# Splitting the queries and keys of two heads on all 128 rows, and laying them over each other by DMA

## The chip, the cores and the metric

The kernel runs on one core of a Trainium2 chip. A time is that of one execution on the device in microseconds (us), the median of several runs; lower is better. The engines are TensorE (PE in the profile), VectorE (DVE), ScalarE (ACT), GpSimd (POOL) and SyncE (SP). Each takes its instructions in order, and semaphores make one wait for another. SBUF is the memory on the core, PSUM holds the results of TensorE in eight banks of 128 rows by 512 floats.

## The reference

Two blocks of a network on 512 tokens of width 2048, in float32. The first is a pooling mixer with a modulation; the second has three attention branches, a gate and an output projection. The change touches the split of queries and keys in two of the branches, of which this matters:

```python
# 64 wide heads: branch A has 12 query and 4 key heads (window), branch B 12 of each (forgetting)
q = rms_norm_2(q, q_gain); k = rms_norm_2(k, k_gain)
A: scores = einsum('bnqkgd,bnskd->bnkgqs', qb, kb) * d**-0.5 + bias        # window of 128, sinks
B: sc = einsum('bqhd,bshd->bhqs', qb, k) * d**-0.5 + cq - c                # causal, c = cumsum(log_f)
out = einsum('...qs,...sd->...qd', softmax(scores), v)
```

## The kernel before

Every float32 product is made of products of high and low parts: a value is cast to float32r (high) and the rest is what the cast left over (low). The stream of weights works like this: SP loads a piece of 128 x 1024 (line 53 and on), ACT casts it to `whi` (line 91), DVE subtracts to `wlo` (line 92), and TensorE multiplies high by high, low by high and high by low (`mm3`, line 260). Two halves of a piece are kept ready beyond the one in use (`take`, line 116). One half serves four banks of output, 12 matmuls.

Beside the projections run the attention units as generators. `aside` puts a generator into a lane, `step` (line 241) is called after every few projection matmuls and adds the lane's rate to a credit; at 1 the generator runs to its next `yield` (rate 0.41 for the units, line 1263). What it issues there stands in each engine's queue at that place. So the order on every engine is fixed when the program is built: a generator with fewer yields comes sooner. There are a unit of kind C, two of kind A (6 heads each) and three of kind B (4 heads each); `drain` ends a unit before the next one's inputs are done.

A unit begins with the head norm (`head_norm`, line 844; L862 and L867 multiply by the norm), then it transposes two heads of 64 at a time: four 128 x 128 transposes on TensorE (L888) into a bank of PSUM, s2 or s3 in turn (line 885), the first head in rows 0 to 63, the second in rows 64 to 127. `transp_stack` (line 882) casts and subtracts from there into the tile `qk12` (12 slots of 128 x 512). For queries a slot holds one head's high part in 64 rows and its low part in the other 64; for keys (kind B only) one slot holds the high part twice, another the low part twice. So one matmul over 128 rows gives high by high plus low by high. Each cast (L892, and L894 for the second copy of keys) and each subtraction (L896) works on 64 rows; an engine can write to other rows than it reads. Keys of kind A go through `transp_split` (L877, L879, L880), whose source has the head doubled already, so it works on all rows; the two calls of a unit take banks s2 and s3 in the same turn.

After that the scores follow (`s0`, line 1049, matmuls at L258 that read `qk12`), the exponentials (L1089), their transposes (`s2`, line 1098, L1111) and the split of the result into `pth` and `ptl` (L1136, L1138), of which there is one tile each (lines 1104 and 1105, 128 x 1280), and the product with the values (`s4`). The profile leaves numbers out of names, so `qk12` and the unsplit input `qk` are both called qk, and the banks s0 to s3 are all s.

Of the kernel before, what the change touches and what calls it, by code (L numbers as in the profile page):

```python
# [8 lines left out]
F32R = mybir.dt.float32r  # L9
AF = mybir.ActivationFunctionType  # L10
# [4 lines left out]
P = 128  # L15
D = 2048
T = 512
# [105 lines left out]
def build(tc, nc, x, vecs, bgate, fg, sinks, bforget, w_mod, w_pin, w_grp, w_pout, mem, w_in, w_kv,  # L123
          w_ba, w_bb, w_bc, w_out, ident, tri, dmask, rel, csel, edge, out):
    es = ExitStack()
    with es:
        _build(es, tc, nc, x, vecs, bgate, fg, sinks, bforget, w_mod, w_pin, w_grp, w_pout, mem, w_in, w_kv,
               w_ba, w_bb, w_bc, w_out, ident, tri, dmask, rel, csel, edge, out)


def _build(es, tc, nc, x, vecs, bgate, fg, sinks, bforget, w_mod, w_pin, w_grp, w_pout, mem, w_in, w_kv,
           w_ba, w_bb, w_bc, w_out, ident, tri, dmask, rel, csel, edge, out):
    V, S, PE = nc.vector, nc.scalar, nc.tensor
    mult, add, sub, vmax, vmin = ALU.mult, ALU.add, ALU.subtract, ALU.max, ALU.min

    def r32(ap):
        return ap.bitcast(F32)
# [85 lines left out]
    def bank(tag, name=None):  # L223
        return psp.tile([P, 512], F32, tag=tag, name=name or tag)
# [137 lines left out]
    b = bank("s3")  # L362
# [139 lines left out]
    for kp in range(8):  # L502
        if kp < 6:
            mem_pair(kp + 2)
        for c in range(2):
# [16 lines left out]
            w = st.whole()  # L522
# [293 lines left out]
    a3 = p3.enter_context(tc.tile_pool(name="a3", bufs=1))  # L816
# [65 lines left out]
    def transp_stack(srcs, outs, gain, keys):  # L882


        b = bank(S4[2 + nside[0] % 2])
        nside[0] += 1
        for i, s in enumerate(srcs):
            PE.transpose(b[:, i * P : (i + 1) * P], s, idf)  # L888
        for e in range(2):
            r, o = slice(64 * e, 64 * e + 64), slice(64 - 64 * e, 128 - 64 * e)  # L890
            hi = outs[e][0]
            S.activation(hi[r, :], b[r, :], AF.Copy, scale=gain[r, :])  # L892
            if keys:
                S.activation(hi[o, :], b[r, :], AF.Copy, scale=gain[r, :])  # L894
            for w in ((r, o) if keys else (o,)):
                V.scalar_tensor_tensor(out=outs[e][1][w, :], in0=b[r, :], scalar=gain[r, :], in1=r32(hi[r, :]), op0=mult, op1=sub)  # L896
            if e or keys:
                yield

    qk12 = a3.tile([P, 12, T], F32R, name="qk12")  # L900
    qkh, qkl = qk12[:, 0:6, :], qk12[:, 6:12, :]
    vhl = a3.tile([P, 2048], F32R, name="vhl")
# [50 lines left out]
    def attend(kind, unit, qk, vz):  # L953
# [12 lines left out]
        def head_state(h):  # L966
            if h not in hs:
                s = {}
                s["nm"] = a3.tile([P, NT], F32, tag="nm", name="nm", bufs=3)
                s["den"] = a3.tile([P, NT], F32, tag="den", name="den", bufs=3)  # L970
                if kind == "B" and "cs" not in s:
                    s["cs"] = a3.tile([P, T], F32R, tag="cst", name="cst", bufs=2)
                    S.activation(s["cs"], r32(ct2), AF.Copy, scale=csl[:, h0 + h : h0 + h + 1])
                hs[h] = s
            return hs[h]

        head_state(0)

        if kind == "C":
            vv = vhl.rearrange("p (m h e) -> p m h e", m=2, h=4)  # L980
# [6 lines left out]
        elif kind == "A":  # L987
            kd = [mkv[:, tt // 2, 512 + 256 * (tt % 2) : 768 + 256 * (tt % 2)].rearrange("p (j e d) -> p j e d", j=2, e=2) for tt in range(NT)]
            vv = vhl[:, :1024].rearrange("p (t h e) -> p t h e", t=NT, h=2)
            zoff = 128  # L990
            silu_z()
            yield from head_norm(qk, 0, 8, 64, k0=6, kdup=kd, beside=split_v([vz[:, tt, :128].rearrange("p (h e) -> p h e", e=64) for tt in range(NT)], [vv[:, tt] for tt in range(NT)], 64))
            for h in range(3):
                outs = [(qk12[:, 2 * h + e, :],) * 2 for e in range(2)]
                yield from transp_stack([qk[:, tt, h * P : (h + 1) * P] for tt in range(NT)], outs, gains[:, 0:1], False)
            for j in range(2):
                transp_split([kd[tt][:, j].rearrange("p a b -> p (a b)") for tt in range(NT)], qk12[:, 6 + 2 * j, :], qk12[:, 7 + 2 * j, :],
                             cols[:, R_KA : R_KA + 1])
                yield
        else:  # L1000
            vv = vhl.rearrange("p (t h e) -> p t h e", t=NT, h=4)
            zoff = 256
            silu_z()
            yield from head_norm(qk, 0, 8, 64, beside=split_v([vz[:, tt, :256].rearrange("p (h e) -> p h e", e=64) for tt in range(NT)], [vv[:, tt] for tt in range(NT)], 64))
            for h in range(4):
                hd = [2 * (h % 2) + e for e in range(2)]
                outs = [(qk12[:, 4 + i, :], qk12[:, 8 + i, :]) if h > 1 else (qk12[:, i, :],) * 2 for i in hd]
                g = gains[:, 1:2] if h < 2 else cols[:, R_KB : R_KB + 1]
                yield from transp_stack([qk[:, tt, h * P : (h + 1) * P] for tt in range(NT)], outs, g, h > 1)
# [242 lines left out]
    for (c0, n), ev in zip(CG[1:], (ev1, ev2)):  # L1252
        cb = [bank(t) for t in M4]
        for kp in range(8):
            tok_tile(cb, 2 * kp, h_h, h_l, kp == 0, kp == 7, n=n, evac=ev)
    drain()
    aside(attend("C", 0, qk, vz), 0.34)
    for kind, unit in (("A", 0), ("A", 1), ("B", 0), ("B", 1), ("B", 2)):
        qk2 = new_qk()
        proj(qk2, False)  # L1260
        vz2 = new_vz()
        proj(vz2, True)
        aside(attend(kind, unit, qk2, vz2), 0.41)
# [153 lines left out]
```

## Time and profile before

| | us |
|---|---|
| median of 3 runs | 2262.62 (2258.87 to 2263.61) |
| the profiled execution | 2262.3 |
| its span, first to last instruction | 2260.5 |
| TensorE busy | 2210.4 (98%) |
| DVE busy | 1146.5 (51%) |
| ACT busy | 883.5 (39%) |
| POOL busy | 0.2 (0%) |

The span is what the profile covers; the execution's own time is 1.8 us longer. Busy time is that of instructions at work. Matmuls overlap, so their durations (0.39 us for 512 columns) are longer than their spacing. In a row, "L892 ACT ACTIVATE qk<-s,gains" is line 892 of the kernel, the engine, the operation, output and inputs; "[0.97 <-DVE qk L896]" says that the engine was idle for 0.97 us before it, and what ended that. SPq is SP's queue of DMA issues.

### The profile page before, as it was taken

To read this page: it belongs to the slowest core of one execution; us is meant where nothing else is said; L and a number is where in the kernel's file an instruction comes from. 1 tells how busy PE (TensorE), PEld (TensorE's weight loads), DVE (VectorE), ACT (ScalarE), POOL (GpSimd) and SP (SyncE) were. 2 spreads that over 40 slices of the span, in tenths; PEclk is the share of its full clock that TensorE was granted. 3 is DMA by queue.
4 is the path that set the end of the run, shared out by engine and by line. 5 is a ranking of instruction groups with operands and counts; after the bars stand their busy time and mean duration, and the time that the engine had idled before them with its cause. 6 is when DMAs were issued, how large, how long until landed. Compare 5 with 4: busy or idle time off the path is not lost.

```text
span 2260.5 us, 26829 instructions
## 1 busy us (share of the span) xinstructions
PE 2210.4 (98%) x10199; PEld 1819.0 (80%) x10199; DVE 1146.5 (51%) x1997; ACT 883.5 (39%) x1719; POOL 0.2 (0%) x4
## 2 busy tenths in 40 slices
PE   7999999999999999999999999999999999999999
PEld 4678888888889988787778787788888888888887
DVE  3676665346665454757564645554334235326333
ACT  4433363333334354545464646442232222224221
POOL 0000000000000000000000000000000000000000
PEclk9989999999999999999999999999999999999999
DMA  9856633347674322222222222233333333333543
GB/s 334 276 164 217 202 99 98 94 122 231 225 224 120 105 75 75 75 75 75 75 75 75 75 75 75 66 98 99 94 93 103 96 100 94 102 94 98 154 131 112
DMA packets 164809, 275.12 MB, mean 122 GB/s; under 512 B 11090, under 2 KB 63048, under 8 KB 164424
## 3 DMA queue, kind: packets, MB, share of 16 engines
q1 hardware_dynamic: 164680, 273.41, 39.6%
q8 instruction: 80, 1.31, 0.2%
q14 instruction: 49, 0.40, 0.1%
HBM read 264.98 MB, written 8.39 MB: 121 GB/s over the span
## 4 chain that ended last, share of the span: by engine, by line
PE 82%; DVE 7%; ACT 5%; DMA 3%; issue 2%; SPq 0%; DVEq 0%; ACTq 0%
PE m L258 53%; PE s L258 26%; DVE wlo L92 2%; DVE qk L896 1%; DMA raw<-w_kv 1%; ACT pt L1089 1%; PE s L1111 1%; ACT whi L91 1%; DMA raw<-w_pout 1%; ACT qk L892 1%; DVE nm L1082 1%; DVE pt L1080 0%; DVE ptl L1138 0%; DVE acc L452 0%; PE colb L258 0%
## 5 line engine op out<-in xcount | busy, mean ns | idle before, releaser
L92 DVE TENSOR_TENSOR wlo<-raw,whi 128x512 fp32r<-128x512 f32 (+2 forms) x740 | 493.4, 675 | 759.6 <-ACT whi L91 744.7
L91 ACT CAST whi<-raw 128x512 fp32r<-128x512 f32 (+2 forms) x740 | 441.4, 608 | 872.5 <-PE m L258 385.4
L258 PE MATMUL m<-whi,h_h 128*128 128x512 f32 (+2 forms) x960 | 373.3, 389 | 1.7 <-ACT whi L91 1.1
L258 PE MATMUL m<-wlo,h_h 128*128 128x512 f32 (+2 forms) x960 | 363.0, 378 | 2.9 <-DVE wlo L92 2.6
L258 PE MATMUL m<-whi,h_l 128*128 128x512 f32 (+2 forms) x960 | 362.6, 378 | 0.0
L258 PE MATMUL m<-h_h,whi 128*128 128x512 f32 x768 | 304.2, 396 | 0.0
L258 PE MATMUL m<-h_h,wlo 128*128 128x512 f32 x768 | 301.4, 392 | 1.2 <-DVE wlo L92 1.2
L258 PE MATMUL m<-h_l,whi 128*128 128x512 f32 x768 | 301.1, 392 | 0.0
L258 PEld LDWEIGHTS m<-wlo,h_h 128*128 128x128 f32 x960 | 181.1, 189 | 31.9 <-DVE wlo L92 6.1
L258 PEld LDWEIGHTS m<-whi,h_l 128*128 128x128 f32 x960 | 180.7, 188 | 31.5
L258 PEld LDWEIGHTS m<-whi,h_h 128*128 128x128 f32 x960 | 181.2, 189 | 28.6 <-ACT whi L91 1.4
L258 PE MATMUL s<-h_h,whi 128*128 128x512 f32 x512 | 200.8, 392 | 0.0
L258 PE MATMUL s<-h_l,whi 128*128 128x512 f32 x512 | 200.4, 391 | 0.0
L258 PE MATMUL s<-h_h,wlo 128*128 128x512 f32 x512 | 200.4, 391 | 0.0
L258 PEld LDWEIGHTS m<-h_h,wlo 128*128 128x128 f32 x768 | 145.4, 189 | 32.6 <-DVE wlo L92 1.7
L258 PEld LDWEIGHTS m<-h_h,whi 128*128 128x128 f32 x768 | 145.6, 190 | 30.3 <-ACT whi L91 0.5
L258 PEld LDWEIGHTS m<-h_l,whi 128*128 128x128 f32 x768 | 145.5, 190 | 29.4
L258 PEld LDWEIGHTS s<-h_h,whi 128*128 128x128 f32 x512 | 97.1, 190 | 20.3
L258 PEld LDWEIGHTS s<-h_l,whi 128*128 128x128 f32 x512 | 97.0, 189 | 20.3
L258 PEld LDWEIGHTS s<-h_h,wlo 128*128 128x128 f32 x512 | 96.9, 189 | 20.3
L258 PE MATMUL m<-whi,y_h 128*128 128x512 f32 x256 | 102.6, 401 | 1.4 <-DVE t L778 1.4
L258 PE MATMUL m<-whi,y_l 128*128 128x512 f32 x256 | 99.9, 390 | 0.0
(239 smaller groups left out, 2739.6 us busy)
## 6 DMA issues: line engine op xcount, KB each, us to landing
raw<-w_mod SPq DMA_DIRECT2D x96, 512.0 KB, 4.3
raw<-w_in SPq DMA_DIRECT2D x96, 512.0 KB, 3.7
raw<-w_pin SPq DMA_DIRECT2D x58, 512.0 KB, 3.8
raw<-w_in SPq DMA_DIRECT2D x96, 256.0 KB, 3.0
raw<-w_pout SPq DMA_DIRECT2D x32, 512.0 KB, 4.4
raw<-w_out SPq DMA_DIRECT2D x32, 512.0 KB, 3.7
raw<-w_in SPq DMA_DIRECT2D x32, 384.0 KB, 3.4
raw<-w_kv SPq DMA_DIRECT2D x16, 512.0 KB, 6.6
```

What stands on the lines that cost most here:

```text
L91: self.nc.scalar.copy(h3, v)
L92: self.nc.vector.tensor_tensor(out=l3, in0=v, in1=h3.bitcast(F32), op=ALU.subtract)
L258: PE.matmul(ps, lhsT=lhsT, rhs=rhs, start=start, stop=stop)
L892: S.activation(hi[r, :], b[r, :], AF.Copy, scale=gain[r, :])
L896: V.scalar_tensor_tensor(out=outs[e][1][w, :], in0=b[r, :], scalar=gain[r, :], in1=r32(hi[r, :]), op0=mult, op1=sub)
L1082: V.tensor_reduce(out=s["nm"][:, qt : qt + m], in_=w, axis=AX.X, op=vmax)
L1089: S.activation(pt[:, c0 : c0 + n], (pt if kind == "A" else b)[:, c0 : c0 + n], AF.Exp, bias=s["nm"][:, qt : qt + 1], accum_out=s["den"][:, ...
L1111: PE.transpose(b[:, x * P : (x + 1) * P], pt[:, c : c + P], idf)
```

## The change

`transp_stack` now casts the whole bank, 128 rows, to a high part and subtracts on 128 rows to a low part. Both go into a free half of `pth` and `ptl` (columns 0 to 511 for the first pair of two, 512 to 1023 for the second); every other pair takes new tiles of these names, which are the same memory again. Then copies, started from POOL's queue, lay each head's 64 rows into `qk12`: two per head for queries, four for keys. There is one yield for every pair, where key pairs had two. Nothing else changes.

```diff
--- before.py
+++ after.py
@@ -886,17 +886,27 @@
         nside[0] += 1
         for i, s in enumerate(srcs):
             PE.transpose(b[:, i * P : (i + 1) * P], s, idf)
+        fresh = not both
+        if fresh:
+            both[:] = [a3.tile([P, 1280], F32R, tag=t, name=t) for t in ("pth", "ptl")]
+        c = slice(0, T) if fresh else slice(T, 2 * T)
+        hi, lo = both[0][:, c], both[1][:, c]
+        S.activation(hi, b, AF.Copy, scale=gain)
+        V.scalar_tensor_tensor(out=lo, in0=b, scalar=gain, in1=r32(hi), op0=mult, op1=sub)
+        if not fresh:
+            both.clear()
         for e in range(2):
             r, o = slice(64 * e, 64 * e + 64), slice(64 - 64 * e, 128 - 64 * e)
-            hi = outs[e][0]
-            S.activation(hi[r, :], b[r, :], AF.Copy, scale=gain[r, :])
             if keys:
-                S.activation(hi[o, :], b[r, :], AF.Copy, scale=gain[r, :])
-            for w in ((r, o) if keys else (o,)):
-                V.scalar_tensor_tensor(out=outs[e][1][w, :], in0=b[r, :], scalar=gain[r, :], in1=r32(hi[r, :]), op0=mult, op1=sub)
-            if e or keys:
-                yield
-
+                for w in (r, o):
+                    nc.gpsimd.dma_start(outs[e][0][w, :], hi[r, :])
+                    nc.gpsimd.dma_start(outs[e][1][w, :], lo[r, :])
+            else:
+                nc.gpsimd.dma_start(outs[e][0][r, :], hi[r, :])
+                nc.gpsimd.dma_start(outs[e][0][o, :], lo[r, :])
+        yield
+
+    both = []
     qk12 = a3.tile([P, 12, T], F32R, name="qk12")
     qkh, qkl = qk12[:, 0:6, :], qk12[:, 6:12, :]
     vhl = a3.tile([P, 2048], F32R, name="vhl")
@@ -975,6 +985,7 @@
             return hs[h]
 
         head_state(0)
+        both.clear()
 
         if kind == "C":
             vv = vhl.rearrange("p (m h e) -> p m h e", m=2, h=4)
```

Line 894 in the changed kernel is the cast, 895 the subtraction, 902 and 903 are the copies of keys, 905 and 906 those of queries; L1100 is what was L1089, L1147 what was L1136.

On ACT, in the first B unit, two query pairs and two key pairs are split between casts of the weight stream. Before:

```order
L892 ACTIVATE qk12_5578<-s2_9396,gains_74 64x512 [waits PE_49]
L892 ACTIVATE qk12_5578<-s2_9396,gains_74 64x512 [waits DVE_49]
L892 ACTIVATE qk12_5578<-s3_9411,gains_74 64x512 [waits PE_49]
L892 ACTIVATE qk12_5578<-s3_9411,gains_74 64x512 [waits DVE_49]
L91 CAST whi_9423<-raw_9276 128x512 [waits Activation_49]
L892 ACTIVATE qk12_5578<-s2_9433,cols_73 64x512 [waits PE_49]
L894 ACTIVATE qk12_5578<-s2_9433,cols_73 64x512
L892 ACTIVATE qk12_5578<-s2_9433,cols_73 64x512 [waits DVE_49]
L894 ACTIVATE qk12_5578<-s2_9433,cols_73 64x512
L91 CAST whi_9455<-raw_9335 128x512 [waits DMAHW7_49,DMAHW0_49,Activation_49]
L892 ACTIVATE qk12_5578<-s3_9465,cols_73 64x512 [waits PE_49]
L894 ACTIVATE qk12_5578<-s3_9465,cols_73 64x512
```

After, at the same place (pth is the buffer, DMASW are the semaphores of copies from POOL):

```order
L91 CAST whi_9409<-raw_9296 128x512 [waits DMAHW5_49,DMAHW6_49,PE_49,Activation_49]
L894 ACTIVATE pth_9421<-s2_9416,gains_74 128x512 [waits PE_49]
L894 ACTIVATE pth_9421<-s3_9435,gains_74 128x512 [waits PE_49]
L91 CAST whi_9449<-raw_9296 128x512 [waits DVE_49]
L894 ACTIVATE pth_9464<-s2_9459,cols_73 128x512 [waits DMASW2_49,DMASW4_49,DMASW0_49,DMASW6_49,DVE_49,PE_49]
L894 ACTIVATE pth_9464<-s3_9485,cols_73 128x512 [waits PE_49]
L91 CAST whi_9500<-raw_9355 128x512 [waits DMAHW7_49,DMAHW0_49]
L983 ACTIVATE cst_9521<-ct2_5581,csl_5572 128x512
L1100 ACT_TABLE_LOAD [waits DVE_49]
```

Twelve casts of 64 rows have become four of 128, and the third of them, with all that stands behind it on ACT, waits for copies. On POOL, which had no instruction between its start and its end, the unit's 24 copies now stand in a row. These are the last two of the second query pair and the first six of the first key pair:

```order
L905 DMA qk12_5578<-pth_9421 64x512 [waits DMASW6_49,PE_49]
L906 DMA qk12_5578<-ptl_9422 64x512 [waits DMASW7_49]
L902 DMA qk12_5578<-pth_9464 64x512 [waits DMASW0_49,Activation_49]
L903 DMA qk12_5578<-ptl_9465 64x512 [waits DMASW1_49,DVE_49]
L902 DMA qk12_5578<-pth_9464 64x512 [waits DMASW2_49]
L903 DMA qk12_5578<-ptl_9465 64x512 [waits DMASW3_49]
L902 DMA qk12_5578<-pth_9464 64x512 [waits DMASW4_49,PE_49]
L903 DMA qk12_5578<-ptl_9465 64x512 [waits DMASW5_49]
```

A copy waits for the cast or the subtraction that it moves, and for the copy issued eight places earlier. On TensorE the first scores of that unit (matmuls on qk12 into bank s0) stood 15 projection matmuls behind the transposes of the last pair, L888, and waited for ACT and DVE. Before, with the last six of the 15:

```order
L258 MATMUL m1_9239<-whi_9423,h_h9_584 128x512
L258 MATMUL m1_9239<-wlo_9424,h_h9_584 128x512
L258 MATMUL m1_9239<-whi_9423,h_l9_600 128x512
L258 MATMUL m2_9240<-whi_9423,h_h9_584 128x512
L258 MATMUL m2_9240<-wlo_9424,h_h9_584 128x512
L258 MATMUL m2_9240<-whi_9423,h_l9_600 128x512
L258 MATMUL s0_9500<-qk12_5578 128x128 [waits Activation_49]
L258 MATMUL s0_9500<-qk12_5578 128x128 [waits DVE_49]
L258 MATMUL s0_9500<-mov_5580,cst_9257 128x128
L258 MATMUL s0_9500<-dmr_5568,idr_5564 128x128
```

After, they stand 6 projection matmuls behind these transposes and wait for copies:

```order
L888 MATMUL s3_9485<-idf_72,qk_8216 128x128 [waits DVE_49]
L888 MATMUL s3_9485<-idf_72,qk_8216 128x128 x3
L258 MATMUL m0_9258<-whi_9409,h_h8_583 128x512 [waits Activation_49]
L258 MATMUL m0_9258<-wlo_9410,h_h8_583 128x512
L258 MATMUL m0_9258<-whi_9409,h_l8_599 128x512
L258 MATMUL m1_9259<-whi_9409,h_h8_583 128x512
L258 MATMUL m1_9259<-wlo_9410,h_h8_583 128x512
L258 MATMUL m1_9259<-whi_9409,h_l8_599 128x512
L258 MATMUL s0_9510<-qk12_5578 128x128 [waits DMASW2_49,DMASW1_49,DMASW0_49]
L258 MATMUL s0_9510<-qk12_5578 128x128 [waits DMASW3_49,DMASW1_49]
L258 MATMUL s0_9510<-mov_5580,cst_9277 128x128
L258 MATMUL s0_9510<-dmr_5568,idr_5564 128x128
```

The scores have come nearer to the pairs that they need, and what they wait for is no longer ACT and DVE but the copies behind these.

## Rows read from the trace of the kernel before

**Rows 1.** The page: busy time of each engine (its first part), and shares by engine of the chain that ended last (its fourth).

```profile
PE 2210.4 (98%) x10199; PEld 1819.0 (80%) x10199; DVE 1146.5 (51%) x1997; ACT 883.5 (39%) x1719; POOL 0.2 (0%) x4
...
PE 82%; DVE 7%; ACT 5%; DMA 3%; issue 2%; SPq 0%; DVEq 0%; ACTq 0%
```

**Rows 2.** Busy time of each engine from 780 to 1480 us, with the number of instructions in brackets; behind it the granted clock as a share of 2.4 GHz, the DMA engines' busy share and GB/s.

```profile
780.00:1480.00 700.00, 677.08 (x3354) 562.61 (x3353) 395.54 (x800) 365.60 (x789) 0.00 (x0) 1.00 0.26 75
```

**Rows 3.** The waits of TensorE from 895 to 1470 us, all eight groups: who waited for whom, us in total, times, longest.

```profile
PE s L1172 <- DVE un L1043: 6.4, 4, 2.2
PE s L1111 <- DVE ptl L1138: 3.7, 2, 2.0
PE s L888 <- DVE qk L862: 3.4, 4, 1.1
PE s L1111 <- ACT pt L1089: 3.2, 3, 1.3
PE m L258 <- DVE wlo L92: 1.8, 3, 0.9
PE s L877 <- DVE qk L896: 1.6, 3, 0.9
PE s L258 <- DVE ptl L1138: 1.6, 2, 0.8
PE m L258 <- ACT qk L840: 0.6, 1, 0.6
```

**Rows 4.** The instructions on the tiles called qk in the whole run: count, shortest, median and longest duration in ns, first and last start, forms. L892 and L894 are casts on 64 rows, L896 subtractions on 64, L879 and L880 the same on 128.

```profile
L892 ACT ACTIVATE qk<-s,gains x24: 682/685/690, 914.9 to 1376.9; 64x512 fp32r<-64x512 f32 x24
L896 DVE SCALAR_TENSOR_TENSOR qk<-s,gains,qk x24: 743/750/756, 915.6 to 1377.7; 64x512 fp32r<-64x512 f32 x24
L896 DVE SCALAR_TENSOR_TENSOR qk<-s,cols,qk x24: 742/750/758, 1152.2 to 1388.7; 64x512 fp32r<-64x512 f32 x24
...
L892 ACT ACTIVATE qk<-s,cols x12: 683/685/687, 1150.8 to 1386.5; 64x512 fp32r<-64x512 f32 x12
L894 ACT ACTIVATE qk<-s,cols x12: 682/684/687, 1151.5 to 1387.2; 64x512 fp32r<-64x512 f32 x12
...
L879 ACT ACTIVATE qk<-s,gains x4: 691/692/692, 810.3 to 817.9; 128x512 fp32r<-128x512 f32 x4
L880 DVE SCALAR_TENSOR_TENSOR qk<-s,gains,qk x4: 750/752/753, 811.1 to 818.6; 128x512 fp32r<-128x512 f32 x4
```

**Rows 5.** The timeline at the start of unit B0: start, duration, instruction. The first query pair's transposes, cast and subtraction, the second pair's transposes, two projection matmuls one behind the other, the two key pairs' transposes and the first scores.

```profile
1144.99 0.62 PE L888 MATMUL s<-idf,qk 128*128 128x128 f32 x4
...
1145.65 0.69 ACT L892 ACTIVATE qk<-s,gains 64x512 fp32r<-64x512 f32 x1 [3.85 <-PE s L888]
...
1146.37 0.74 DVE L896 SCALAR_TENSOR_TENSOR qk<-s,gains,qk 64x512 fp32r<-64x512 f32 x1 [0.54 <-ACT qk L892]
...
1146.85 0.60 PE L888 MATMUL s<-idf,qk 128*128 128x128 f32 x4
...
1147.98 0.40 PE L258 MATMUL m<-whi,h_h 128*128 128x512 f32 x1
...
1148.21 0.39 PE L258 MATMUL m<-wlo,h_h 128*128 128x512 f32 x1
...
1148.77 0.63 PE L888 MATMUL s<-idf,qk 128*128 128x128 f32 x4
...
1152.69 0.60 PE L888 MATMUL s<-idf,qk 128*128 128x128 f32 x4
...
1156.58 0.34 PE L258 MATMUL s<-qk 128*128 128x128 f32 x2
```

**Rows 6.** The timeline at the start of unit A0: the first pair's cast, the third pair's transposes, and the transposes of the two pairs of keys, with the idle time before them.

```profile
914.92 0.69 ACT L892 ACTIVATE qk<-s,gains 64x512 fp32r<-64x512 f32 x1 [5.04 <-PE s L888]
...
918.63 0.60 PE L888 MATMUL s<-idf,qk 128*128 128x128 f32 x4
...
921.04 0.63 PE L877 MATMUL s<-idf,mkv 128*128 128x128 f32 x4 [0.41 <-DVE qk L896]
...
924.06 0.63 PE L877 MATMUL s<-idf,mkv 128*128 128x128 f32 x4 [0.30 <-DVE qk L896]
```

**Rows 7.** DMA: the page's row of the only queue with data; of the table of issues (KB each, median us from issue to landing) the two kinds of 128 KB in numbers and the load of rels, 128 KB; and that load's issue on SP in the timeline (start, duration).

```profile
q1 hardware_dynamic: 164680, 273.41, 39.6%
...
raw<-w_in SPq DMA_DIRECT2D x32, 128.0 KB, 2.4
...
out_dram<-g SPq DMA_DIRECT2D x2, 128.0 KB, 1.9
rels<-rel SPq DMA_DIRECT2D x1, 128.0 KB, 2.6
...
717.64 0.43 SPq L824 DMA_DIRECT2D rels<-rel  x1
```

**Rows 8.** Busy time in stretches of 2 us from 956 us on, in the order of columns of rows 2; the granted clock stands behind the count for POOL.

```profile
956.00:958.00 2.00, 2.00 (x13) 1.74 (x12) 1.89 (x5) 0.00 (x0) 0.00 (x0) 1.00 0.00 0
958.00:960.00 2.00, 0.46 (x4) 0.25 (x3) 0.69 (x4) 1.58 (x7) 0.00 (x0) 1.00 0.00 0
960.00:962.00 2.00, 1.39 (x6) 1.33 (x7) 1.97 (x5) 0.58 (x2) 0.00 (x0) 0.63 0.04 8
962.00:964.00 2.00, 2.00 (x6) 1.58 (x5) 1.77 (x4) 0.66 (x3) 0.00 (x0) 0.52 0.28 66
964.00:966.00 2.00, 2.00 (x16) 1.86 (x15) 0.69 (x1) 0.94 (x3) 0.00 (x0) 1.00 0.73 197
```

## The prediction, made before the changed kernel was run

> **What bounds the kernel now.** I read the page's first and fourth parts first. TensorE is busy 98% of the span and carries 82% of the chain that ended last, most of it in the projection matmuls [rows 1]; ACT and DVE are busy 39% and 51%. So work taken off ACT or DVE counts only where TensorE waits for it, and anything that makes TensorE wait counts in full. Next comes the stretch in which the attention units run beside the projections: from 780 to 1480 us TensorE is busy 677.08 of 700 us, and POOL does nothing there [rows 2]. The waits of TensorE alone, from 895 to 1470 us (the five units that use transp_stack), come to 22.3 us in eight groups [rows 3]: that is all that relief of ACT and DVE could ever return. Of it, 1.6 us is a wait for the subtractions that change (L877 for L896); 3.4 us waits for the head norm (L862), which stays. Last I read the split itself, instruction by instruction [rows 4 to 6].
>
> **What is removed.** A pass over 64 rows takes as long as one over 128: the cast 0.685 us against 0.692, the subtraction 0.750 against 0.752 [rows 4]. There were 24 + 12 + 12 = 48 casts and 24 + 24 = 48 subtractions; 18 pairs of heads (3 in each of two A units, 4 in each of three B units) now need 18 of each. So 30 × 0.685 = 20.6 us leave ACT and 30 × 0.75 = 22.5 us leave DVE. Nearly all of that lay beside TensorE's projections. What I count is the wait for a PSUM bank in an A unit, 0.41 + 0.30 = 0.7 us before the key transposes [rows 6]: 2 × 0.7 = 1.4 us gained. In a B unit the two yields that go bring the first scores forward by 15 projection matmuls; these are then done later, so that is worth nothing in itself, but it takes away time in which the copies could have run.
>
> **What is added.** POOL issues 4 copies for a query pair and 8 for a key pair: 2 × 3 × 4 + 3 × (2 × 4 + 2 × 8) = 96 copies of 64 rows by 2 KB, 128 KB each. They make three new waits. (a) The first scores wait for copies. (b) The third pair of a unit takes a fresh pair of the buffers pth and ptl, of which there is one each, so its cast on ACT and its subtraction on DVE wait until the eight copies of the first two pairs have landed; behind them on the same engines stand the casts and subtractions of the weights, and the PSUM bank. (c) The first head's own pth waits for the copies of the last pairs.
>
> **The price of a copy.** No DMA of before leaves from POOL: the page has one queue of data, SP's [rows 7]. The nearest rows: SP spends 0.43 us on issuing a 128 KB load, and loads of this size land 2.4 us (32 of them) or 2.6 us after issue, a store 1.9 us [rows 7]. So the price on POOL lies between 0.43 us (as SP's) and 2.4 us (each lands before the next goes out). I take 1.0 us, which is as many times 0.43 as 2.4 is of it (√(0.43 × 2.4) = 1.02), and landing 2.0 us after the issue ends (2.4 − 0.43). Below nothing it can't lie: POOL's queue is in order.
>
> The Trainium skill ("DMA: Bandwidth & Descriptors", section Latency and other measured facts) gives about 1 us to the first byte on POOL's path, where descriptors are made by software, and about 0.6 us on SP's. By that difference an issue would be an estimated 0.43 + 0.4 = 0.83 us, and the end, on a straight line between the two sums below, about 2297; no run here shows a POOL copy yet.
>
> **A B unit, worked through (unit B0).** The first pair's cast ends at 1145.65 + 0.69 = 1146.34 [rows 5]. Copies 1 to 8 then go out back to back from 1146.4 to 1154.4, since the second pair, transposed at 1146.85, is split by 1149. The seventh (last high part) lands at 1155.4, the eighth at 1156.4. The third pair's cast runs 1155.4 to 1156.1, its subtraction 1156.4 to 1157.15. Copy 9 goes at 1156.1, copy 10 at 1157.15, copy 12 ends at 1160.15 and lands at 1162.15. TensorE reaches the first scores much earlier: third pair's transposes from 1148.77 to 1149.4, 9 matmuls at 0.23 us (the spacing in [rows 5]) = 2.05, the fourth pair's transposes 0.45, 6 matmuls 1.4: 1153.3. It waits 8.9 us, and all projections queue behind that matmul. Then wait (c): copies 13 to 24 end at 1172.15 and land at 1174.15; the second transposes into bank s2 come 36 matmuls (8.2 us) and four small groups (2.9 us) after the first scores, at 1173.25, and need two subtractions after 1174.15, so 1174.9: 1.6 us more. ACT blocked from about 1149 to 1155.4 holds back weight casts, but each feeds 12 matmuls (2.7 us) and two are ready ahead, so this hides under the 8.9 us.
>
> The clock comes on top. After TensorE had been idle for 1.54 of 2 us, the granted clock fell to 0.63 and 0.52 in the next two stretches of 2 us, that is down to the 1.2 GHz level for most of them, and was back at 1.00 behind them [rows 8]. That loses 2 × 0.37 + 2 × 0.48 = 1.7 us, and I count it once for every wait of 2 us or more. B unit: 8.9 + 1.6 + 1.7 = 12.2 us, three times 36.6 us.
>
> **An A unit (A0).** The first cast ends at 914.92 + 0.69 = 915.6 [rows 6], copies 1 to 8 go out until 923.65, the last lands at 925.65, and the third pair's subtraction ends at 926.4. The keys are split into two banks in turn, and the second key's transposes want the third pair's bank; without the two waits of before they would come at 924.06 − 0.71 = 923.35. So 3.0 us of wait, 1.7 us of clock, 0.7 us gained: 4.0 us, twice 8.0 us. The first scores need the first pair and the keys only; they are not held.
>
> **Sum.** 36.6 + 8.0 = 44.6 us. The profiled execution took 2262.3 us (span 2260.5), 0.3 under the median 2262.62, so nothing is to be corrected: 2262.3 + 44.6 = 2307 us.
>
> **The ends of the price.** At 0.43 us: in B0 copy 8 waits for the second pair's subtraction and ends at 1150.25, lands at 1152.2, copy 12 lands at 1156.3, a wait of 3.0 us and 1.7 us of clock; (c) is gone. In A0 the third pair is ready at 922.9, before it is wanted. 3 × 4.7 − 1.4 = 12.7: 2275 us. At 2.4 us: in B0 copy 12 lands at about 1176 and copy 24 at 1204.8, waits of 22.7 and 18.4 us, 3.4 us of clock; in A0 12.3 + 1.0. 3 × 44.5 + 2 × 13.3 = 160: 2422 us.
>
> **Rivals.**
> *POOL issues as fast as SP*: 2275 us by the line above. For it: the transfers are alike and the DMA engines are only a quarter busy (0.26, [rows 2]). Against: nothing shows POOL at that pace.
> *DVE holds POOL up*: if an issue on POOL must wait for the DVE instruction that is running, with DVE busy 395.54 of 700 us [rows 2] and 0.75 us long, a copy costs 1.0 + 0.56 × 0.75 = 1.4 us. Copy 12 then lands at 1166.55 (13.3 us of wait), (c) is 6.5 us, clock 3.4; A 7.3 us: 3 × 23.2 + 2 × 7.3 = 84, 2346 us. Against: no row shows DVE and POOL at work together, and a wait behind every DVE instruction is the most it could be. The Trainium skill ("SBUF — State Buffer", section Who interferes with whom) has such a lock between DVE and descriptor making on POOL, but for copies and scalar operations in a two-port mode, and infers that a two-operand subtraction does not hold it; no trace here shows either.
> *The relief of ACT and DVE decides, and the kernel is not slower*: if copies cost next to nothing, TensorE gains its waits for the casts and subtractions beside them: 1.6 + 1.8 (weights) + 3.7 + 3.2 (the heads' transposes) = 10.3 us [rows 3], so 2252 us. It decides from the point at which the first scores of a B unit are not held. That needs two landings and a subtraction between the second pair's split (1148.95) and 1153.3, 4.35 us; with the shortest landing row, 1.9 us, and issues for nothing, it is 1.9 + 0.75 + 1.9 = 4.55 us. So even then there is no room: little chance.
> *It does not do what it says* (for instance each copy of a key pair could be done without): the order shows the copies and the waits as told, so I give this nothing.
>
> **Chances.** Forecast (a copy at about 0.6 to 1.2 us, 2285 to 2330 us): 0.50. As fast as SP (2265 to 2285): 0.20. DVE in the way, or dearer still up to 1.6 us: 0.15; one landing at a time, above 2370: 0.05. Relief or copies all hidden: 0.10, half of it past 0.2%. 0.2% (4.5 us) is about what a measurement here can tell from no change. So faster 0.05, the same 0.05, slower 0.90. The range, 2267 to 2360, leaves out the serial case and about half of the gains and of the dearest copies.
>
> **What the profile after would show.** POOL's DMA rows with their spacing: 1.0 us if I am right. TensorE waiting on its L258 scores for DMA in each B unit, some 9 us, three times (after 1150, 1265, 1380), and on L877 in each A unit, some 3 us; ACT's L894 idle for some 6 us before the third pair, released by a DMA; a granted clock near 0.5 just behind these waits. Wrong I would be if the scores wait for nothing, or if the time goes at weight casts instead; a time under 2267 means that copies land faster than any row of before.

## The result, and the profile after

The changed kernel takes 2296.34 us (median of 4 runs, 2293.23 to 2298.55), the kernel before beside it 2263.11: a ratio of 1.0149, 95% interval 1.0131 to 1.0167, or 33.2 us more. The profiled execution took 2293.23 us, its span is 2291.5. It is slower, as forecast, inside the range and 11 us under the 2307 of the prediction.

From the page: busy time, the chain that ended last, and the two DMA queues that move data (packets, MB, share of 16 engines' span).

```profile
PE 2216.4 (97%) x10199; PEld 1825.4 (80%) x10199; DVE 1123.6 (49%) x1967; ACT 863.8 (38%) x1691; POOL 49.2 (2%) x100
...
q1 hardware_dynamic: 164680, 273.41, 39.1%
q0 software_dynamic: 7680, 12.59, 2.7%
...
PE 78%; issue 11%; DVE 4%; DMA 3%; ACT 3%; POOL 1%; SPq 0%; DVEq 0%; ACTq 0%; POOLq 0%
```

Against [rows 1], ACT lost 19.7 us and DVE 22.9 us of work, close to the 20.6 and 22.5 counted: relief on engines that were little waited for. In the chain that ended last TensorE's share fell from 82% to 78%, and "issue", time for which the profile shows no wait, rose from 2% to 11%.

To see where the time went, cut the stretch at the first transposes (L888) of each unit, and the last unit at the first projection's result read from s (L1306). These are the same points of both programs. The busy times of after, in the columns of [rows 2]; units A0, A1, B0, B1, and B2 with what follows it:

```profile
910.58:1028.88 118.30, 109.99 (x556) 91.72 (x555) 69.96 (x155) 55.88 (x128) 6.25 (x12) 0.99 0.33 85
1028.88:1149.51 120.63, 110.76 (x558) 92.19 (x557) 71.13 (x153) 56.88 (x130) 6.13 (x12) 0.99 0.31 84
1149.51:1268.96 119.45, 111.42 (x543) 92.80 (x542) 56.60 (x120) 54.92 (x126) 12.23 (x24) 0.97 0.36 97
1268.96:1391.27 122.31, 113.67 (x545) 94.19 (x544) 57.14 (x121) 55.45 (x127) 12.19 (x24) 0.96 0.37 94
1391.27:1543.67 152.40, 138.73 (x648) 114.39 (x647) 69.54 (x135) 72.10 (x149) 12.20 (x24) 0.96 0.36 95
```

The same view of before gives 116.26, 115.81, 111.90, 114.77 and 141.11 us, with TensorE busy 110.30, 109.33, 110.01, 111.54 and 135.82. So the units grew by 2.0, 4.8, 7.6, 7.5 and 11.3 us, 33.2 in all, which is the whole difference of the medians. TensorE's idle time (length less busy) grew by 2.4, 3.4, 6.1, 5.4 and 8.4 us, 25.7 together; its busy time by the other 7.6 us, the same matmuls at a lower clock.

The waits of TensorE from 895 to 1530 us answer [rows 3]:

```profile
PE s L258 <- DMA qk<-pth: 22.3, 3, 8.2
PE s L877 <- DVE ptl L895: 7.5, 2, 4.3
PE s L1183 <- DVE un L1054: 6.3, 4, 2.2
PE s L888 <- DVE qk L862: 3.5, 4, 1.1
PE s L258 <- ACT pth L1147: 2.0, 1, 2.0
...
PE s L258 <- DMA qk<-ptl: 1.2, 3, 0.6
```

The first is new, and the second has grown from 1.6 us: the first scores of the three B units wait for copies, and the second key's transposes of the two A units for the third pair's bank. Unit B0 shows how, beside [rows 5] (start, duration, instruction, idle time before it; the first cast, copies 1, 2, 7 and 8, the fourth pair's transposes, the third and fourth pair's casts, copy 9, the first score and the second):

```profile
1150.18 0.69 ACT L894 ACTIVATE pth<-s,gains 128x512 fp32r<-128x512 f32 x1 [3.85 <-PE s L888]
...
1151.16 0.51 POOL L905 DMA_DIRECT2D qk<-pth  x1 [105.73 <-ACT pth L894]
...
1151.94 0.52 POOL L906 DMA_DIRECT2D qk<-ptl  x1 [0.28 <-DVE ptl L895]
...
1154.59 0.54 POOL L905 DMA_DIRECT2D qk<-pth  x1
1155.09 0.54 POOL L906 DMA_DIRECT2D qk<-ptl  x1
...
1155.72 0.60 PE L888 MATMUL s<-idf,qk 128*128 128x128 f32 x4
1159.74 1.27 ACT L894 ACTIVATE pth<-s,cols 128x512 fp32r<-128x512 f32 x2 [6.54 <-DMA qk<-pth]
...
1160.95 0.52 POOL L902 DMA_DIRECT2D qk<-pth  x1 [5.31 <-ACT pth L894]
...
1164.90 0.44 PE L258 MATMUL s<-qk 128*128 128x128 f32 x1 [7.18 <-DMA qk<-pth]
...
1165.75 0.45 PE L258 MATMUL s<-qk 128*128 128x128 f32 x1 [0.41 <-DMA qk<-ptl]
```

POOL needs half a microsecond for a copy and had issued the first eight by 1155.6. But the third pair's cast could start only at 1159.74: the seventh copy, issued at 1154.59, had taken 5.0 us to land. Over all query copies of a high part, with how long an issue took (ns) and from issue to landing (us, shortest, median, longest):

```profile
L905 POOL DMA_DIRECT2D qk<-pth x24: 512/519/649, 913.6 to 1397.2; - x24
...
DMA to landing us min/median/max: 2.2/2.7/6.8
```

Stretches of 2 us show what stood in the way and what followed (columns of [rows 2]):

```profile
1155.00:1157.00 2.00, 2.00 (x12) 1.66 (x11) 0.00 (x0) 0.00 (x0) 0.63 (x2) 1.00 1.06 282
1157.00:1159.00 2.00, 0.72 (x4) 0.24 (x2) 0.00 (x0) 0.00 (x0) 0.00 (x0) 1.00 1.17 248
1159.00:1161.00 2.00, 0.00 (x0) 0.00 (x0) 0.53 (x1) 1.25 (x3) 0.05 (x1) 1.00 0.09 12
1161.00:1163.00 2.00, 0.00 (x0) 0.00 (x0) 1.47 (x3) 1.14 (x3) 1.77 (x4) 0.86 0.40 82
1163.00:1165.00 2.00, 0.10 (x1) 0.13 (x1) 0.00 (x0) 0.00 (x0) 1.88 (x5) 0.50 0.92 216
1165.00:1167.00 2.00, 1.59 (x7) 1.43 (x8) 0.00 (x0) 0.00 (x0) 2.00 (x5) 0.50 0.98 217
1167.00:1169.00 2.00, 2.00 (x7) 1.71 (x7) 0.62 (x2) 0.78 (x1) 2.00 (x5) 0.50 1.04 240
```

From 1155 to 1159 us POOL issues little, yet all 16 DMA engines are full (1.06 and 1.17): the copies share them with weight loads from SP's queue. By queue, from 1155 to 1159 us (packets, MB, share of 16 engines; q0 is the copies', q1 SP's):

```profile
q0 software_dynamic: 337, 0.53, 61.3%
q1 hardware_dynamic: 544, 0.52, 50.3%
```

Then both ACT and DVE, and at last TensorE, stand. When TensorE resumes at 1164.90, it does so at the 1.2 GHz level (0.50), until about 1169.

### The profile page after: what moved, and what is told of

It reads as the page before. It is cut to its first block, busy times and chain, and to the rows that moved or that the text cites. A ratio compares the mean times of both kernels' runs of the same rounds, so it can differ in the third digit from the quotient of the medians.

```text
span 2291.5 us, 26980 instructions
## 1 busy us (share of the span) xinstructions
PE 2216.4 (97%) x10199; PEld 1825.4 (80%) x10199; DVE 1123.6 (49%) x1967; ACT 863.8 (38%) x1691; POOL 49.2 (2%) x100
## 4 chain that ended last, share of the span: by engine, by line
PE 78%; issue 11%; DVE 4%; DMA 3%; ACT 3%; POOL 1%; SPq 0%; DVEq 0%; ACTq 0%; POOLq 0%
PE m L258 50%; PE s L258 26%; DMA raw<-w_kv 1%; DVE wlo L92 1%; PE s L1122 1%; DVE acc L452 1%; DMA qk<-ptl 0%; ACT whi L91 0%; DMA raw<-w_pout 0%; ACT pt L1100 0%; PE colb L258 0%; POOL qk L906 0%; DMA nat<-mem 0%; PE s L748 0%; POOL qk L905 0%
## 5 line engine op out<-in xcount | busy, mean ns | idle before, releaser
L92 DVE TENSOR_TENSOR wlo<-raw,whi 128x512 fp32r<-128x512 f32 (+2 forms) x740 | 493.6, 676 | 773.0 <-ACT whi L91 758.0
L91 ACT CAST whi<-raw 128x512 fp32r<-128x512 f32 (+2 forms) x740 | 441.4, 609 | 878.9 <-PE m L258 390.1
```

The costliest lines, as they stand in the source:

```text
L91: self.nc.scalar.copy(h3, v)
L92: self.nc.vector.tensor_tensor(out=l3, in0=v, in1=h3.bitcast(F32), op=ALU.subtract)
```

## The experiments

Two theories at first. Theory 1: the loss is a chain of two landings of some 3 us through the one pair of buffers (waits (a) and (b) of the prediction). Rival: the copies are limited by what the DMA engines move. Beside them stands a question that the prediction answered with "worth nothing": the order, with its missing yields.

**Own buffers for the third and fourth pair.** The third pair goes into the two tiles called pt, the fourth into sq and os.

```diff
-        hi, lo = both[0][:, c], both[1][:, c]
...
+            tags = ("pt", "pt") if n == 2 else ("sq", "os")
+            hi, lo = (a3.tile([P, T], F32R, tag=t, name="st" + t, bufs=2 if t == "pt" else 1) for t in tags)
```

> The third and fourth pair of a unit get buffers of their own (the tiles pt, sq and os, idle there), so the third pair no longer waits until the first eight copies have landed. Theory 1 (the loss is a chain of two landings through the one pair of buffers, each some 3 us): copies 9 to 12 go out by 1157.2 and land by 1160, TensorE reaches the first scores at 1157.7, so the wait falls from 7.2 to 2.3 us in each B unit, the waits of 3.2 and 4.3 us in the A units go, and with the clock the time falls by about 27 us against the changed kernel, to 2269. Rival (the copies are limited by what the DMA engines move, 0.65 us of all 16 for a copy and more beside weight loads): copy 12 can't land before 1161 to 1162.5 whatever the buffer, a wait of 4 to 5 us stays in each B unit, and the time falls by about 19 us, to 2277. If the buffer is not the cause at all: 2296.

Measured: 2287.6 us, ratio 1.0109 (1.0092 to 1.0126). Neither time came. On the wait the rival was right: it is 4.8, 4.6 and 5.6 us, since copy 11, the last that the first score needs, landed only at about 1164.8, 12.9 us after the first transposes (1151.96), though the buffer held nothing up. But the time fell by 8.7 us, not 19: in the five units TensorE's idle time fell by 13.7 us, while its busy time grew by 3.5 (588.05 instead of 584.57). The tiles that I borrowed are wanted soon: all waits of ACT and DVE for a copy out of them, in the whole run,

```profile
ACT L1106 <- DMA qk<-stsq: 15.0, 2, 7.7
...
DVE pt L1097 <- DMA qk<-stpt: 4.3, 2, 2.1
```

hold up the exponentials and, in each A unit, the first DVE instruction that writes pt. What these waits cost in time is not shown by itself. A0 stayed at 118.3 us although its L877 wait was gone: TensorE is busy 1.35 us longer in it (111.34 instead of 109.99).

**Half of every copy.**

```diff
-                    nc.gpsimd.dma_start(outs[e][0][w, :], hi[r, :])
+                    nc.gpsimd.dma_start(outs[e][0][w, 0:256], hi[r, 0:256])
```

(and so the other three)

> Every copy moves only the first 256 of the 512 columns, so half the queries and keys stay what they were before, and the scores of these are of old data; the number of copies, issues and waits is the same. Rival (DMA engines): the first eight copies land at about 1157.8 instead of 1159.7 in unit B0, the last four of the needed twelve 1 us sooner as well, the wait of 7.2 us falls to about 4.4, that of the A units to under 2, and the time falls by about 16 us, to 2280. Theory 1 with a landing time that does not depend on the load: no change, 2296.

Measured: 2285.78 us, 1.0108 (1.009 to 1.0125), between the two. L905 copies land after 2.0 us (median) instead of 2.7, but the longest still takes 4.5, and the third pair's cast in B0 comes 9.3 us after the first transposes (1161.95 less 1152.68) instead of 10.2. So bytes are only a part: something else holds a few copies up.

**No weight loads**, before and after the change: the load of each piece is left out and the first piece read again.

```diff
+        if self.same(self.plan[self.nd]):
+            if self.keep is not None:
+                self.raws[self.nd] = self.keep
...
+                return
```

> The kernel before without the weight loads of the A and B projections: 79 of their 80 pieces of 512 KB are not loaded, and the first is used again in their place, so the output is another. All other work is done. Expected 2262, within 3 us, since no wait of TensorE for a weight load is seen there. It is the base for the next run.

> The changed kernel, likewise without these weight loads (output as in the run before this one). If the copies land late because weight loads stand before them in the DMA engines (copies 6 to 8 of unit B0 land 3.3 to 4.1 us after their issue, the first five 2.0 to 2.4 after theirs): all land about 2 us after issue, the third pair's cast in B0 comes some 2 us sooner, so do the last four of the twelve copies that are needed, the waits of 7.2 us fall to about 5 and those of the A units to about 1.5, and the difference to the run before this one is 20 to 25 us. If weight loads have no part in it: 33 us as between the whole kernels. If all of the loss were that contention: under 10 us.

Measured: 2262.92 us before (1.0001, 0.9991 to 1.0011) and 2287.53 after (1.0112, 1.0097 to 1.0127): a difference of 24.6 us instead of 33.2, in the range expected. Copy 7 of B0 lands 2.9 us after its issue instead of 5.0 (with loads, the trace has copies 6 to 8 landing after 4.2 to 5.1 us, not the 3.3 to 4.1 of the expectation), and the third pair's cast comes 8.1 us after the first transposes (1152.74 less 1144.65), 2.1 sooner; the scores wait 17.8 us in all instead of 22.3, the A units 2.2 instead of 7.5. But the 8.6 us between the two differences are not the whole price of sharing the DMA engines, because the weights that stream beside unit B2 are not among those left out. Units B0 and B2 of the changed kernel without the loads (columns of [rows 2]):

```profile
1144.65:1262.04 117.39, 111.37 (x543) 92.70 (x542) 56.52 (x120) 54.83 (x126) 12.23 (x24) 0.97 0.13 28
...
1381.41:1534.85 153.44, 140.11 (x648) 115.42 (x647) 69.62 (x135) 72.25 (x149) 12.24 (x24) 0.94 0.35 94
```

In B0 the DMA engines' share falls from 0.36 to 0.13, but in B2 it is 0.35 as against 0.36, and B2 is 13.9 us longer than in the kernel before without loads, where the loss with loads was 11.3. In the other four units together the loss falls from 21.9 to 10.7 us. So where the loads are gone, about half of the loss goes with them. The other half needs no loads: the two rounds of copies, and the order.

**The second yield back in the changed kernel, and taken out of the kernel before.**

```diff
                 nc.gpsimd.dma_start(outs[e][0][o, :], lo[r, :])
         yield
+        if keys:
+            yield
```

> The changed kernel with the second yield for each key pair back, so that 15 projection matmuls instead of 6 stand between the last transposes and the first scores, and 9 more ahead of the fourth pair. If the copies then run beside them (theory 1 and the rival alike): the wait falls from 7.2 to 3.8 us, three times 3.4 us, 10 us in all: 2286. If moving the scores is worth nothing because the work that is done ahead is missing later, at the drain that ends a unit: 2296.

```diff
-            if e or keys:
+            if e:
                 yield
```

> The kernel before with one yield for a key pair instead of two, nothing else. The first scores then come 15 projection matmuls sooner, at about 1153.2 in unit B0, when the first key pair's casts and subtractions (1150.8 to 1153.9) are just done. If the order costs nothing by itself: 2263, within 3 us. If the lost yields are themselves a part of the loss (the scores wait for DVE, the unit has less cover): 2266 to 2275.

Measured: 2287.33 us (1.0108, 1.009 to 1.0127), so 9.0 us come back, near the 10 expected if copies run beside the matmuls, though the first scores still wait 5.3, 3.8 and 8.0 us instead of 3.8 each:

```profile
PE s L258 <- DMA qk<-pth: 12.4, 3, 4.9
...
PE s L258 <- DMA qk<-ptl: 4.8, 3, 3.1
```

That is 6.3 us less than the 23.5 of the changed kernel; the rest is in other waits and in the clock. And 2277.04 us (1.0063, 1.0046 to 1.008) for the kernel before with one yield, 14.4 us slower with no copy in it. The second is over what I had expected even for a cost. All of it lies in the B units (116.7, 118.6 and 147.1 us long). B0 there, from 1158 us:

```profile
1158.00:1160.00 2.00, 1.29 (x7) 0.80 (x5) 0.83 (x2) 1.96 (x4) 0.00 (x0) 1.00 0.00 0
1160.00:1162.00 2.00, 0.86 (x3) 0.49 (x4) 1.94 (x4) 0.39 (x1) 0.00 (x0) 1.00 0.00 0
1162.00:1164.00 2.00, 1.14 (x5) 0.43 (x3) 0.06 (x1) 1.85 (x4) 0.00 (x0) 0.63 0.00 0
1164.00:1166.00 2.00, 2.00 (x6) 1.53 (x7) 1.11 (x2) 0.86 (x3) 0.00 (x0) 0.50 0.00 0
1166.00:1168.00 2.00, 2.00 (x6) 1.52 (x6) 0.75 (x3) 1.45 (x4) 0.00 (x0) 0.50 0.64 171
1168.00:1170.00 2.00, 2.00 (x8) 1.62 (x7) 1.31 (x3) 0.40 (x2) 0.00 (x0) 0.66 0.26 91
```

The first scores come 3.4 us sooner after the unit's first transposes, but the last of the twelve casts of the split ends only 0.75 us sooner, and the weights' casts and the exponentials queue behind them. TensorE waits 0.7 us for L91 (to 1159.82) and 1.1 for L92 (to 1161.46), then the clock falls (0.63 from 1162 to 1164, so at about 1162.5), and a wait of 0.9 us for L1089 comes behind it. Of the 4.8 us by which B0 is longer, 3.1 are busy time (113.14 instead of 110.01).

**A units as before, B units as after.** `transp_rows` is the function of the kernel before under another name.

```diff
-                yield from transp_stack([qk[:, tt, h * P : (h + 1) * P] for tt in range(NT)], outs, gains[:, 0:1], False)
+                yield from transp_rows([qk[:, tt, h * P : (h + 1) * P] for tt in range(NT)], outs, gains[:, 0:1], False)
```

> The A units split as before the change, the B units as after it. By the lengths of the units in the two traces (A0 118.3 against 116.3 us, A1 120.6 against 115.8) the A units have 6.9 us of the loss: 2289.5. If the waits of an A unit only stand in for others later: 2296. If the A units hold more than their lengths show (the clock): 2284 or less.

Measured: 2286.6 us, 1.011 (1.0096 to 1.0124). The A units hold 9.7 us, the B units 24.2. That is 3 us more for A than their lengths say; 1.3 of it is that A0 of the profiled execution before has a fall of the clock in it [rows 8] that this run's A0 (115.0 us) has not, and the rest is within the intervals of the two ratios (some 3 to 4 us each way).

**All three mended, and two of the three.** The third pair's buffers are sq and os, the fourth's the half of mkv that is idle in B units; key pair one is split second; the yield is back.

```diff
-            for h in range(4):
+            for h in (0, 2, 1, 3):
                 hd = [2 * (h % 2) + e for e in range(2)]
```

> The changed kernel with three things mended at once: the second yield for each key pair back, buffers of their own for the third and fourth pair (sq and os, and for the last key pair the half of mkv that is idle in the B units), and in the B units the first key pair split second, so that the first scores need the first eight copies only. If the loss is the copies that the first scores and the third pair wait for, and the order: no first scores wait, the B units take 112 to 115 us again (141 to 143 for the last with its end), the A units 116 to 118, and the time is 2258 to 2268. If the copies cost something wherever they stand (by sharing the DMA engines with the weight loads, or by holding up DVE): 2275 or more, with TensorE waiting for weights, or for copies of later heads.

> As the run with all three mended, but the pairs again in the order of the changed kernel (both query pairs, then both key pairs): buffers of their own and the second yield alone. Copy 12 landed 12.9 us after the first transposes of unit B0 where the third pair had its own buffer; with two yields TensorE comes to the first scores 11.6 us after them. So a wait of 1 to 1.5 us in each B unit, too short to cost clock: 2256 to 2262. If the order of the pairs is what made the difference: 2270 or more.

> Buffers of their own and the first key pair split second, but one yield for a key pair as in the changed kernel. The first scores need eight copies, of which the last lands some 9.5 us after the first transposes; TensorE comes to them after 8.2 us. If only copies count: a wait of 1 to 1.5 us in each B unit, 2256 to 2262. If the missing yields cost by themselves, as the kernel before with one yield says (14 us, in the B units): 2266 to 2272.

> The second yield and the first key pair second, but all pairs through the one pair of buffers as in the changed kernel. The third pair then waits for twelve copies, and holds up ACT and DVE with the weights behind it; the first scores are not held by copies, but TensorE waits for weights. A units as in the changed kernel (7 to 10 us over the kernel before). 2265 to 2276 if the buffer is a cause of its own; 2255 to 2262 if it is not.

| kernel | us | ratio to before, 95% interval |
|---|---|---|
| all three | 2253.13 | 0.9962, 0.9949 to 0.9975 |
| without the new order of pairs | 2261.19 | 0.9997, 0.9987 to 1.0007 |
| without the second yield | 2269.15 | 1.0028, 1.0016 to 1.0040 |
| without buffers of their own | 2281.04 | 1.0085, 1.0068 to 1.0102 |
| none (the changed kernel) | 2296.34 | 1.0149, 1.0131 to 1.0167 |

The gains do not add up one by one: buffers of their own, there partly in other tiles, brought back 8.7 us alone and the yield 9.0, the two together 35. With all three the split on 128 rows is faster than both kernels, by 9 us against the one before, and below the range that I had given. Its waits of TensorE from 895 to 1530 us:

```profile
PE s L1193 <- DVE un L1064: 6.3, 4, 2.2
PE s L888 <- DVE qk L862: 3.4, 4, 1.1
PE s L1132 <- DVE ptl L1159: 2.7, 2, 2.1
PE s L258 <- DMA qk<-pth: 1.7, 1, 1.7
PE s L258 <- DVE ptl L1159: 1.7, 2, 0.9
PE m L258 <- DVE wlo L92: 0.8, 2, 0.4
PE s L258 <- DMA qk<-ptl: 0.2, 1, 0.2
```

That is 16.8 us instead of the 22.3 of [rows 3], and unit B0 takes 109.7 us with the clock at 1.00 all through:

```profile
1143.28:1252.96 109.68, 109.26 (x543) 91.28 (x541) 56.48 (x120) 55.20 (x126) 12.25 (x24) 1.00 0.45 106
```

All copies are still there, and the high parts of keys land even later than in the changed kernel (median 5.8 us instead of 3.3), but only one first score waits for them. Without the new order the scores wait 6.8 us for the third pair's copies: 2.1, 1.7 and 3.0 in the three B units, where 1 to 1.5 was expected. The time is in the range expected, but the clock does fall there: it is 0.99 in B0, and TensorE is busy 111.3 us instead of 109.3. Without the second yield they wait 8.7 us (5.2 and 3.5), more than the 1 to 1.5 in each unit that the copies alone were to cost. The time is that of the other theory, but not its mechanism: TensorE's waits for weights, 6.5 us in the kernel before with one yield, are 1.1 here. Against the run with all three, TensorE is idle 8.0 us longer in the five units and busy 7.9 longer: waits for copies, and the clock behind them. Without the buffers the time was over the range that I had expected. ACT's waits for copies there:

```profile
ACT pth L894 <- DMA qk<-pth: 31.8, 4, 9.6
ACT pth L1149 <- DMA qk<-pth: 10.6, 3, 4.2
```

The second line is wait (c) of the prediction, the first head's own pth behind the last copies; TensorE then waits 9.8 us in all for the split (L1124), 6.1 of them in B0 and B1 (2.6 and 3.5), where the kernel before has no such wait.

**The order of pairs in the kernel before.** The same line, in the kernel before.

> The kernel before with the first key pair split second in the B units, nothing else. If what the kernel with all three mended gained over the kernel before (9 us) is the relief of ACT and DVE by the split on 128 rows: 2262, within 3 us. If it is the order of the pairs, which would help without any copies: 2253 to 2257.

Measured: 2262.64 us, 0.9997 (0.9988 to 1.0006). The order alone gains nothing. What the mended kernel has over the one before is then left to the split on 128 rows, that is to the relief of ACT and DVE; this is by elimination. Its five units are 10.5 us shorter (589.35 instead of 599.85): TensorE is idle 5.9 us less in them and busy 4.6 us less.

## Why the prediction was right, and which terms were off

The direction and the places were right: 24.2 us in the B units and 9.7 in the A units were measured (36.6 and 8.0 were forecast), by the waits named, with ACT's L894 idle 6.5 us before the third pair (some 6 forecast). But the loss is a quarter smaller than forecast, 33.2 instead of 44.6 us, and that it came as near as that is in part luck. By its steps:

- *What is removed*: right in work, and right that it counts for little while TensorE waits for copies. But it is not nothing: by elimination the mended kernel shows it as 9 us, near the 10.3 that the relief rival read from [rows 3], though only 5.5 of it are waits (16.8 instead of 22.3 us) and the rest is busy time. That rival needed copies that nobody waits for, and those can be had by order and buffers, not by a faster copy.
- *The price of a copy* was split wrongly. An issue takes 0.52 us, not 1.0, nearest to SP's 0.43 [rows 7]; a landing takes 2.2 to 7.0 us, not the issue and 2.0. The two errors met: the third cast in B0 came 9.6 us after the first (1159.74 less 1150.18), where 9.75 was forecast. The agreement is luck, and the rival "as fast as SP" was right on the issue and still wrong by 21 us in the time, because it left the landings at 2 us. What made landings late has no term in the sum at all: copies that queue behind each other and behind weight loads on the DMA engines, which the prediction took from a mean over 700 us to be a quarter busy [rows 2].
- *Wait (a)* was 7.2, 6.9 and 8.2 us, 8.9 forecast. From copy 9's issue to the first score it took only 3.95 us (1160.95 to 1164.90), 6.05 forecast (1156.1 to 1162.15): the issues are quicker, and the first score starts on the eleventh copy; the twelfth holds up the second score, by another 0.4 us.
- *Wait (c)*, 1.6 us in each B unit, did not come: with issues of half the length the last copies are in time. It came where copies 13 to 24 start late, in the run without buffers of their own.
- *The A units*: waits of 3.2 and 4.3 us, 3.0 forecast, by the same two errors as in B0. The key transposes that wait for the third pair's subtraction came 11.4 us after the unit's first cast (923.95 less 912.56), 11.5 forecast (926.4 less 914.92).
- *The clock*: 5 × 1.7 = 8.5 us forecast, 7.6 of more busy time measured, but by units −0.3, 1.4, 1.4, 2.1 and 2.9 instead of 1.7 each. In A0 the execution before had a fall of its own [rows 8], and in B1 and B2 it cost more.
- *Left out*: waits of before that vanish. L1111 for the exponentials, 3.2 us [rows 3], has no row after.
- *The yields*, "worth nothing in itself" but less cover for the copies: the cover was in the sum, and the 9.0 us of the run with the yield back are near 3 × 3.4. But in the kernel before the same shift costs 14.4 us, so the first half of the sentence is wrong. In the changed kernel TensorE waits for copies at that place, and how much of those 14.4 us its loss contains is not shown.

The Trainium skill ("DMA: Bandwidth & Descriptors", section Latency and other measured facts) led to an estimate of 0.83 us for an issue on POOL and 2297 us in all. The time agrees, by the same luck, but the trace does not agree with the way to it: POOL issues in 0.52 us and the time goes in the landing. By "SBUF — State Buffer", section Who interferes with whom, DVE was not expected to hold POOL up with a two-operand subtraction; the trace agrees, since a DVE subtraction takes 0.75 us beside POOL's issues as it did without them, and the issues have a median of 0.52 us all through.

What stays open: which copy stood behind which load, since the shares and the run without loads show the sum only; what sharing costs in unit B2, where no run is without loads; and why the clock falls behind one short wait and not behind another. The wait of 2.2 us for un in A0 is in both traces, and only the execution before shows the fall.

## What to carry to other kernels

A copy that replaces work on an idle engine brings a latency where there was none, and it is judged by who waits for it: with 96 copies the split cost 33 us where the next step stood behind them, and gained 9 us where order, yields and buffers put other work in between. Before moving a step nearer to its consumer, ask what else is queued between the two on every engine. And price a DMA by two numbers, the issue and the landing, the second at the share of the DMA engines that the rest of the kernel leaves free.

## What the hardware showed that I had not expected

- A copy of 64 rows by 2 KB out of POOL's queue takes 0.52 us to issue and lands 2.2 us after issue at the least, 2.7 to 3.5 at the median and 7.0 at the longest; with half the bytes the shortest are 1.8 us. Half the bytes did not halve the wait: the first scores still wait 15.5 us instead of 22.3.
- Copies issued every half microsecond are limited by what moves them even without loads: from 1163 to 1169 us of the changed kernel they alone hold 97.7% of the 16 engines at 224 GB/s, and from copy 9 to copy 24 of B0 the time from issue to landing grows from 2.2 to 3.8 us.
- The granted clock stayed at 1.00 for more than 4 us into TensorE's idle time in B0 (from 1157.7), fell to 0.50 while it was still idle, and stayed there for 4 us after work had begun again. The pauses of the changed kernel are thus charged twice, and the second charge looks like busy time: 7.6 of the 33.2 us.
- A fall of the clock does not need one long wait: in B0 of the kernel before with one yield it follows two waits of 0.7 and 1.1 us, and the unit's busy time grows by more (3.1 us) than its idle time (1.6 us).
